# One encoder layer in split fp32r: the hi passes of a weight piece first, its lo passes last, and one score step moved up

## Chip, core and metric

The kernel runs on one core of one Trainium2 chip. The metric is device time in microseconds for one execution, the smaller the better. The inputs are drawn once, and the whole layer is computed in one launch.

## What is computed

One layer of a bidirectional encoder over 256 tokens of width 4096, all in float32:

```
h = layer_norm(x, emb_ln_g, emb_ln_b)
p = h @ w_in                      # 4096 x (4*2048 + 2048 + 512 + 512 + 2048)
y_conv = c_b * centred_short_conv(c_c * c_h, conv_w) * silu(c_z)
y_attn = banded_window_attention(a_q, a_k, a_v, sink) * silu(a_z)
y = concatenate([y_conv, y_attn]) @ w_out          # 4096 x 4096
out = layer_norm(2**0.25 * h + y, ln_g, ln_b)
```

The attention has 16 query heads and 4 key/value heads of size 128, a window of 128 tokens to both sides, a linear distance bias and a learned sink logit in each softmax. The convolution has three taps.

## The kernel before

**Split products.** TensorE multiplies fp32r operands. To keep float32 accuracy, each operand is split in two fp32r halves, hi and lo, and each product is three matmuls into the same PSUM accumulator: hi by hi, hi by lo, lo by hi. The stationary operand is a 128x128 block of the activations (`xT`, with the hi half in its first 256 columns and the lo half in the next 256). The moving operand is 128x256 out of a weight piece (`whi` and `wlo`).

**Pieces.** The weights come in pieces of 128x2048 from HBM into raw buffers (`w0` to `w2`, sometimes more). The work is a list of 376 steps, one for each piece: 302 for the input projection (26 chunks of 512 columns) and 74 for the output projection (7 chunks of 512 and 2 of 256). There are three kinds:

- a plain piece ("in", "out"): 4 blocks of 128 rows by 512 columns, 48 matmuls, written by `mm` (L251 to L253) and `mm_out` (L921 to L923);
- a half piece ("half"): 2 such blocks, 24 matmuls, also by `mm`;
- a pair ("pair", "opair"): one level of Winograd's form of Strassen's product over two blocks of rows, two column halves and two token halves. It has seven products instead of eight, 21 matmuls, written by `mm_pair` (L275 to L277), into the accumulators `acc` and `pacc`. VectorE first makes sums of the raw weights (`sums`, L183 to L185); sums of the activations lie in `SC`.

**Halves of a piece.** ScalarE copies the raw piece into `whi` (`split_hi`, L204), rounded to fp32r. VectorE subtracts this from the raw piece and gets `wlo` (`split_lo`, L208). There are three buffers each of `whi` and `wlo`. The raw buffer is free when `wlo` is made, and SyncE's queue then loads the next piece.

**Order.** It is written by hand: engines take their instructions in program order, and waits follow from the operands. At step j the matmuls of piece j are issued, then `split_hi(j + 3)`, then the other work that is due at step j (a table `later`, filled by `at`), then loads, `sums(j + 4)` and `split_lo(j + 3)`.

**Attention between the pieces.** Four heads at a time are worked off in the steps behind a chunk of queries. `SPREAD` names the step of each part: transposed queries (`q_tr`, `q_lo`) and for each head `scores` (L561 to L563), `s_add` (L568 and the two instructions behind it: bias, maximum, negation), `exps`, `recip`, `norms`, `p_tr` (L602: transposes of the probabilities, and L604, their hi half), `p_lo` (L609, their lo half), `pv` (L616 to L618, the product with v, six matmuls) and `out_z`. Scores, transposed probabilities and the output of `pv` share two PSUM buffers, `att`. Transposes of projections are on L491.

**End.** The output projection's last chunk is worked token half by token half, and the final normalisation is applied at once.

Of the kernel before, what the change touches and what calls it, by code (L numbers as in the profile page):

```python
# [8 lines left out]
F32 = mybir.dt.float32  # L9
# [5 lines left out]
P = 128  # L15
D = 4096
S = 256
KT = D // P
# [14 lines left out]
W = 512  # L33
PK = PIECE // W
# [6 lines left out]
HW = W // 2  # L41
# [46 lines left out]
def npairs(ci):  # L88
    return PAIRS[ci] if ci < OUT else OUT_ORDERS[ci - OUT].count("S")
# [11 lines left out]
def encoder_kernel(ctx: ExitStack, tc: tile.TileContext, x, emb_g, emb_b, wi, ws, conv_w, sink, wo, ln_g, ln_b, out):  # L101
    nc = tc.nc
# [5 lines left out]
    ps_acc = ctx.enter_context(tc.tile_pool(name="ps_acc", bufs=4, space=PSUM))  # L108
# [115 lines left out]
    xT = const.tile([P, KT, 2 * S], F32R, name="xT")  # L224
# [9 lines left out]
    acc = {}  # L234

    def mm(j):
        _, ci, q = steps[j]
        hi, lo = wh.pop(j), wl.pop(j)
        first = j == 0 or steps[j - 1][1] != ci
        last = j == N_IN - 1 or steps[j + 1][1] != ci  # L240
        pk, k0 = (2, 2 * q) if steps[j][0] == "half" else (PK, q * PK)
        for k in range(pk):
            kt = k0 + k
            for i in range(2):
                if first and k == 0:
                    acc[ci, i] = ps_acc.tile([P, W], F32, name="acc")
                a = acc[ci, i]
                xh, xl = xT[:, kt, i * P:(i + 1) * P], xT[:, kt, S + i * P:S + (i + 1) * P]
                for c in range(0, W, HW):
                    o, sl = a[:, c:c + HW], slice(k * W + c, k * W + c + HW)  # L250
                    nc.tensor.matmul(o, xh, hi[:, sl], start=(first and k == 0 and c == 0), stop=False)  # L251
                    nc.tensor.matmul(o, xh, lo[:, sl], start=False, stop=False)  # L252
                    nc.tensor.matmul(o, xl, hi[:, sl], start=False, stop=(last and k == PK - 1 and c > 0))  # L253

    pacc, SC = {}, None

    def mm_pair(j):


        _, ci, p = steps[j]  # L260
        hi, lo = (t.pop(j).rearrange("p (b w) -> p b w", w=HW) for t in (wh, wl))
        last = p == npairs(ci) - 1
        if p == 0:
            for k in range(2):
                pacc[ci, k] = ps_p.tile([P, 2, HW], F32, name="pacc")
        a, b = 2 * p, 2 * p + 1
        x = lambda kt, i: (xT[:, kt, i * HT:(i + 1) * HT], xT[:, kt, (2 + i) * HT:(3 + i) * HT])
        sc = lambda n: (SC[p][:, 0, n, :], SC[p][:, 1, n, :])
        p0, p1, c0, c1 = pacc[ci, 0], pacc[ci, 1], acc[ci, 0], acc[ci, 1]
        for (ah, al), w, o, opens, closes in (  # L270
                (x(a, 0), 2, p0[:, 0, :], True, False), (x(b, 0), 3, c0[:, 0:HW], False, False),
                (sc(2), 1, c0[:, HW:W], False, False), (x(b, 1), 7, c1[:, 0:HW], False, False),
                (sc(0), 5, p1[:, 1, :], True, False), (x(a, 1) if ci < OUT else sc(3), 6, p0[:, 1, :], False, True),
                (sc(1), 4, p1[:, 0, :], False, True)):
            nc.tensor.matmul(o, ah, hi[:, w, :], start=(opens and p == 0), stop=False)  # L275
            nc.tensor.matmul(o, ah, lo[:, w, :], start=False, stop=False)  # L276
            nc.tensor.matmul(o, al, hi[:, w, :], start=False, stop=(closes and last))  # L277


    def small_chain(i, dst):  # L280
# [10 lines left out]
    with tc.tile_pool(name="pro", bufs=1) as pro:  # L291
# [15 lines left out]
        first = [wpool.tile([P, PIECE + GAP], F32, name=f"first{j}", tag="whi")[:, OFF:OFF + PIECE] for j in range(2)]  # L307
# [117 lines left out]
        load(6)  # L425
        transp2(4)
        mm(2)
        turned2(4)
        x_split(4)
        split(4)  # L430
        load(7)
        transp2(5)
        mm(3)
        turned2(5)
        x_split(5)
        split(5)
        load(8)
        transp2(6)
        mm(4)
        turned2(6)  # L440
        x_split(6)
# [58 lines left out]
    v = pa.tile([P, 2, 2, 2, P], F32R, name="v")  # L500
# [110 lines left out]
    def pv(h):  # L611
        t, g = st_.pop(("pT", h))[0], h // GROUP % 2
        o_ps = st_["o", h] = ps_att.tile([P, S], F32, name="att")
        for kb in range(2):
            vh, vl = v[:, g, kb, 0, :], v[:, g, kb, 1, :]
            nc.tensor.matmul(o_ps, vh, t[:, 0, kb, :], start=(kb == 0), stop=False)  # L616
            nc.tensor.matmul(o_ps, vh, t[:, 1, kb, :], start=False, stop=False)
            nc.tensor.matmul(o_ps, vl, t[:, 0, kb, :], start=False, stop=(kb == 1))  # L618

    def out_z(h):  # L620
        y = st_["zT", h // GROUP][:, h % GROUP, :]
# [4 lines left out]
    def head(n, *steps):  # L626
        return [(t, f, n) for t, f in zip(steps, (scores, s_add, exps, recip, norms, p_tr, p_lo, pv, out_z))]

    SPREAD = [(6, q_tr, 0), (7, q_lo, 0), (10, q_tr, 1), (11, q_lo, 1)] + head(0, 8, 9, 9, 10, 10, 13, 15, 19, 20) + head(
        1, 9, 10, 10, 11, 12, 19, 21, 22, 23) + head(2, 13, 18, 18, 19, 20, 24, 27, 28, 29) + head(  # L630
        3, 21, 22, 22, 23, 23, 28, 30, 31, 32)

    def open_pc():
# [169 lines left out]
    for j in range(n_pro, N_IN):  # L803
        kind, ci, q = steps[j]
        if j == z0 + 4:
            extra.clear()
        if j == z0 + 12:
            extra.insert(0, (pw, "w6"))
        mm_pair(j) if kind == "pair" else mm(j)
        split_hi(j + 3)  # L810
        for fn, a in later.pop(j, []):
            fn(*a)
        if kind == "pair" and q == PAIRS[ci] - 1:
            pair_copy(ci)
            at(j + 1, pair_sums, ci)
        if j in X_SUMS:
            x_sums(X_SUMS.index(j), pa.tile([P, 4 * S], F32, name="xs", tag="zT", bufs=2))
        if steps[j + 1][1] != ci or j == N_IN - 1:
            if ci == c_ch0:
                at(j + 10, open_pc)  # L820
            if PAIRS[ci]:
                at(j + (4 if j < N_IN - 1 else 1), chunk_end, j + 1, ci)
            else:
                chunk_end(j, ci)
        loads(j)
        sums(j + 4)
        split_lo(j + 3)
# [79 lines left out]
    def mm_out(j, n, halves, k0=0, k1=None):  # L907
        c0, w, pk, j0 = chunks[n]
        ci, q = steps[j][1:]
        hi, lo = wh[j], wl[j]  # L910
        for k in range(k0, k1 or pk):
            s = q * pk + k
            first, last = j == j0 and k == 0, s == KT - 1
            for i in halves:
                if first:
                    acc[ci, i] = ps_acc.tile([P, 512], F32, name="acc")[:, 0:w]
                o = acc[ci, i]
                yh, yl = xT[:, s, i * P:(i + 1) * P], xT[:, s, S + i * P:S + (i + 1) * P]
                for c in range(0, w, HW):
                    oc, sl = o[:, c:c + HW], slice(k * w + c, k * w + c + HW)  # L920
                    nc.tensor.matmul(oc, yh, hi[:, sl], start=(first and c == 0), stop=False)  # L921
                    nc.tensor.matmul(oc, yh, lo[:, sl], start=False, stop=False)  # L922
                    nc.tensor.matmul(oc, yl, hi[:, sl], start=False, stop=(last and c + HW == w))  # L923

    def plus_res(n):

# [84 lines left out]
    for n, (c0, w, pk, j0) in enumerate(chunks):  # L1011
        us = out_units(n)
        np_ = sum(u[0] == "opair" for u in us)
        for t, (kind, _, q) in enumerate(us):
            j = j0 + t
            if kind == "opair":
                mm_pair(j)
            else:
                mm_out(j, n, (0,) if n == ncs - 1 else (0, 1))
# [35 lines left out]
    n = ncs - 1  # L1055
    r0 = finish_lhs(n, 0)
    mm_out(last_mm, n, (1,))
    mm_out(last_mm + 1, n, (1,))
    finish_tr(0)
    end_out2(n, 0, r0)  # L1060
# [73 lines left out]
```

## Time and profile before

| | |
|---|---|
| time, median of 3 runs | 1524.67 us (1524.48 to 1525.1) |
| profiled execution, its own time | 1524.95 us |
| its span, first to last instruction | 1523.2 us |
| granted TensorE clock, mean | 0.999 |
| ScalarE busy | 783.4 us (51%) |
| VectorE busy | 1329.8 us (87%) |
| HBM read over the span | 305.23 MB, 206 GB/s together with what is written |

In the profile, PE is TensorE's matmuls, PEld its weight loads, DVE VectorE, ACT ScalarE. Times are microseconds from the start of the span. A row of the timeline has the start, the length, the engine, the line of the kernel, the operation, its output and inputs, the shapes, how many were merged into the row, and in brackets the idle time ahead of it with what ended it. Matmuls are pipelined: the length of one reaches over the starts of the next two, so the step from start to start is what counts, not the length. The list of waits names who waited for whom, the total, how often, and the longest.

### The profile page before, as it was taken

Reading aid. Unit: us, or ns where it says so; the run is one execution under the profiler, and the core shown is the slowest. Engines: PE = TensorE matmul, PEld = TensorE weight load, DVE = VectorE, ACT = ScalarE, POOL = GpSimd, SP = SyncE. Lnnn points to the kernel's source line nnn. Section 1 sums busy time; section 2 is a strip of 40 time slices with the busy share of each in tenths; the row PEclk is TensorE's granted clock in tenths of the full one; section 3 lists DMA queues with packets and bytes.
Section 4 is the critical chain, followed back from the end, with each engine's and each line's share of the span. In section 5 each row is a group of like instructions: output and inputs, shape, how many; then the busy total and the mean of one; then the engine's idle time right before and its main releaser. Section 6 shows DMA issues by size and latency. Waiting matters only on the chain.

```text
span 1523.2 us, 29953 instructions
## 1 busy us (share of the span) xinstructions
PE 1501.5 (99%) x12947; PEld 1478.8 (97%) x12947; DVE 1329.8 (87%) x1555; ACT 783.4 (51%) x669; POOL 1.3 (0%) x7
## 2 busy tenths in 40 slices
PE   7999999999999999999999999999999999999998
PEld 4999999999999999999999999999999999999997
DVE  7769899899899899899898989999899688888876
ACT  4545546656566555545455455545456444443431
POOL 0000000000000000000000000000000000000000
PEclk9999999999999999999999999999999999999999
DMA  7555654656655555656556555556557756666563
GB/s 289 211 180 194 208 199 165 205 180 204 203 178 184 176 184 200 236 194 231 188 191 208 204 211 194 196 193 234 201 201 278 281 190 229 247 213 227 215 238 143
DMA packets 71748, 316.17 MB, mean 208 GB/s; under 512 B 8544, under 2 KB 12608, under 8 KB 50880
## 3 DMA queue, kind: packets, MB, share of 16 engines
q1 hardware_dynamic: 70608, 312.43, 58.7%
q8 instruction: 101, 1.65, 0.4%
q10 hardware_dynamic: 1008, 1.84, 0.3%
q14 instruction: 31, 0.25, 0.0%
HBM read 305.23 MB, written 8.91 MB: 206 GB/s over the span
## 4 chain that ended last, share of the span: by engine, by line
PE 79%; DVE 15%; ACT 3%; issue 2%; DMA 1%; SPq 0%; ACTq 0%; DVEq 0%
PE acc L252 13%; PE acc L253 12%; PE acc L251 12%; DVE wlo L208 9%; PE acc L922 6%; PE acc L923 6%; PE acc L921 6%; PE pacc L277 4%; PE pacc L276 4%; PE pacc L275 4%; PE acc L277 3%; PE acc L275 3%; PE acc L276 3%; ACT whi L204 3%; DVE w L183 2%
## 5 line engine op out<-in xcount | busy, mean ns | idle before, releaser
L204 ACT ACTIVATE whi<-w 128x2048 fp32r<-128x2048 f32 (+1 forms) x354 | 623.8, 1762 | 615.6 <-DVE w L185 220.0
L208 DVE TENSOR_TENSOR wlo<-w,whi 128x2048 fp32r<-128x2048 f32 (+1 forms) x354 | 736.7, 2083 | 121.9 <-ACT whi L204 121.3
L252 PE MATMUL acc<-wlo,xT 128*128 128x256 f32 x1976 | 547.7, 277 | 3.7 <-DVE wlo L208 3.2
L251 PE MATMUL acc<-whi,xT 128*128 128x256 f32 x1976 | 547.0, 277 | 0.0
L253 PE MATMUL acc<-whi,xT 128*128 128x256 f32 x1976 | 544.5, 276 | 0.0
L252 PEld LDWEIGHTS acc<-wlo,xT 128*128 128x128 f32 x1976 | 371.1, 188 | 8.7 <-DVE wlo L208 8.2
L251 PEld LDWEIGHTS acc<-whi,xT 128*128 128x128 f32 x1976 | 371.1, 188 | 0.0
L253 PEld LDWEIGHTS acc<-whi,xT 128*128 128x128 f32 x1976 | 371.0, 188 | 0.0
L922 PE MATMUL acc<-wlo,xT 128*128 128x256 f32 x848 | 233.5, 275 | 1.0 <-DVE wlo L208 1.0
L921 PE MATMUL acc<-whi,xT 128*128 128x256 f32 x848 | 233.6, 275 | 0.0
L923 PE MATMUL acc<-whi,xT 128*128 128x256 f32 x848 | 233.3, 275 | 0.0
L922 PEld LDWEIGHTS acc<-wlo,xT 128*128 128x128 f32 x848 | 159.2, 188 | 1.4 <-DVE wlo L208 1.4
L921 PEld LDWEIGHTS acc<-whi,xT 128*128 128x128 f32 x848 | 159.2, 188 | 0.4 <-issue 0.4
L923 PEld LDWEIGHTS acc<-whi,xT 128*128 128x128 f32 x848 | 159.2, 188 | 0.0
L183 DVE TENSOR_TENSOR w<-w 128x512 f32<-128x512 f32 x179 | 122.5, 684 | 8.0 <-DMA w<-in_ws 8.0
L275 PE MATMUL acc<-whi,xT 128*128 128x256 f32 x370 | 102.1, 276 | 0.0
L276 PE MATMUL acc<-wlo,xT 128*128 128x256 f32 x370 | 102.1, 276 | 0.0
L277 PE MATMUL acc<-whi,xT 128*128 128x256 f32 x370 | 102.0, 276 | 0.0
L275 PE MATMUL pacc<-whi,xT 128*128 128x256 f32 x350 | 98.1, 280 | 0.0
L276 PE MATMUL pacc<-wlo,xT 128*128 128x256 f32 x350 | 96.5, 276 | 0.0
L277 PE MATMUL pacc<-whi,xT 128*128 128x256 f32 x350 | 96.4, 276 | 0.0
L277 PE MATMUL pacc<-whi,SC 128*128 128x256 f32 x330 | 90.9, 275 | 0.0
(230 smaller groups left out, 2047.0 us busy)
## 6 DMA issues: line engine op xcount, KB each, us to landing
w<-in_wi SPq DMA_DIRECT2D x112, 1024.0 KB
w<-in_ws SPq DMA_DIRECT2D x202, 512.0 KB
w<-in_wo SPq DMA_DIRECT2D x41, 1024.0 KB
R<-in_wo SPq DMA_DIRECT2D x13, 1024.0 KB
x<-in_x SPq DMA_DIRECT2D x7, 512.0 KB
yl<-yd SPq DMA_DIRECT2D x7, 512.0 KB
xc<-in_x SPq DMA_DIRECT2D x14, 256.0 KB
R<-in_ws SPq DMA_DIRECT2D x6, 512.0 KB
```

Source lines behind the costliest of these rows:

```text
L183: nc.vector.tensor_tensor(s01, b22, b12.to_broadcast([P, 2, HW]), op=ALU.add)
L204: nc.scalar.activation(part(j, wh[j]), part(j, raw[j]), AF.Copy)
L208: nc.vector.tensor_tensor(part(j, wl[j]), part(j, raw[j]), part(j, wh[j]).bitcast(F32), op=ALU.subtract)
L251: nc.tensor.matmul(o, xh, hi[:, sl], start=(first and k == 0 and c == 0), stop=False)
L252: nc.tensor.matmul(o, xh, lo[:, sl], start=False, stop=False)
L253: nc.tensor.matmul(o, xl, hi[:, sl], start=False, stop=(last and k == PK - 1 and c > 0))
L275: nc.tensor.matmul(o, ah, hi[:, w, :], start=(opens and p == 0), stop=False)
L276: nc.tensor.matmul(o, ah, lo[:, w, :], start=False, stop=False)
L277: nc.tensor.matmul(o, al, hi[:, w, :], start=False, stop=(closes and last))
L921: nc.tensor.matmul(oc, yh, hi[:, sl], start=(first and c == 0), stop=False)
L922: nc.tensor.matmul(oc, yh, lo[:, sl], start=False, stop=False)
L923: nc.tensor.matmul(oc, yl, hi[:, sl], start=False, stop=(last and c + HW == w))
```

## The change

In `mm`, `mm_pair`, `mm_out` and `pv`, the loop over the halves of the moving operand becomes the outermost one. First come all matmuls of the step with the hi half as moving operand (with both the hi and the lo half of the stationary operand), then all with the lo half. Number and shapes stay. In `SPREAD`, `s_add` of head 2 goes from step 18 to step 17.

```diff
 def mm(j):                        # mm_out in the same way
-        for k in range(pk):
-            kt = k0 + k
...
-                for c in range(0, W, HW):
-                    o, sl = a[:, c:c + HW], slice(k * W + c, k * W + c + HW)
-                    nc.tensor.matmul(o, xh, hi[:, sl], start=(first and k == 0 and c == 0), stop=False)
-                    nc.tensor.matmul(o, xh, lo[:, sl], start=False, stop=False)
-                    nc.tensor.matmul(o, xl, hi[:, sl], start=False, stop=(last and k == PK - 1 and c > 0))
+        for w, offs in ((hi, (0, S)), (lo, (0,))):
+            for k in range(pk):
+                for i in range(2):
+                    for off in offs:
+                        x = xT[:, k0 + k, off + i * P:off + (i + 1) * P]
+                        for c in range(0, W, HW):
+                            nc.tensor.matmul(acc[ci, i][:, c:c + HW], x, w[:, k * W + c:k * W + c + HW],
+                                             start=(first and w is hi and k + off + c == 0),
+                                             stop=(last and w is lo and k == PK - 1 and c > 0))
 def mm_pair(j):
+        for (ah, al), w, o, opens, _ in products:
             nc.tensor.matmul(o, ah, hi[:, w, :], start=(opens and p == 0), stop=False)
-            nc.tensor.matmul(o, ah, lo[:, w, :], start=False, stop=False)
-            nc.tensor.matmul(o, al, hi[:, w, :], start=False, stop=(closes and last))
+            nc.tensor.matmul(o, al, hi[:, w, :], start=False, stop=False)
+        for (ah, _), w, o, _, closes in products:
+            nc.tensor.matmul(o, ah, lo[:, w, :], start=False, stop=(closes and last))
 def pv(h):
         for kb in range(2):
-            vh, vl = v[:, g, kb, 0, :], v[:, g, kb, 1, :]
-            nc.tensor.matmul(o_ps, vh, t[:, 0, kb, :], start=(kb == 0), stop=False)
-            nc.tensor.matmul(o_ps, vh, t[:, 1, kb, :], start=False, stop=False)
-            nc.tensor.matmul(o_ps, vl, t[:, 0, kb, :], start=False, stop=(kb == 1))
+            for part_ in range(2):
+                nc.tensor.matmul(o_ps, v[:, g, kb, part_, :], t[:, 0, kb, :], start=(kb + part_ == 0), stop=False)
+        for kb in range(2):
+            nc.tensor.matmul(o_ps, v[:, g, kb, 0, :], t[:, 1, kb, :], start=False, stop=(kb == 1))
 SPREAD
-        1, 9, 10, 10, 11, 12, 19, 21, 22, 23) + head(2, 13, 18, 18, 19, 20, 24, 27, 28, 29) + head(
+        1, 9, 10, 10, 11, 12, 19, 21, 22, 23) + head(2, 13, 17, 18, 19, 20, 24, 27, 28, 29) + head(
```

More of the change, by code (lines that the diff above doesn't have):

```diff
@@ L241, in mm @@
         pk, k0 = (2, 2 * q) if steps[j][0] == "half" else (PK, q * PK)
-        for k in range(pk):
-            kt = k0 + k
+        if first:
             for i in range(2):
[L245 to L248, printed above, removed]
-                for c in range(0, W, HW):
-                    o, sl = a[:, c:c + HW], slice(k * W + c, k * W + c + HW)
-                    nc.tensor.matmul(o, xh, hi[:, sl], start=(first and k == 0 and c == 0), stop=False)
-                    nc.tensor.matmul(o, xh, lo[:, sl], start=False, stop=False)
-                    nc.tensor.matmul(o, xl, hi[:, sl], start=False, stop=(last and k == PK - 1 and c > 0))
+                acc[ci, i] = ps_acc.tile([P, W], F32, name="acc")
+        for w, offs in ((hi, (0, S)), (lo, (0,))):
[7 more added lines that the diff above has]
+                                             stop=(last and w is lo and k == PK - 1 and c > 0))
     pacc, SC = {}, None
@@ L269, in mm_pair @@
         p0, p1, c0, c1 = pacc[ci, 0], pacc[ci, 1], acc[ci, 0], acc[ci, 1]
-        for (ah, al), w, o, opens, closes in (
+        products = (
                 (x(a, 0), 2, p0[:, 0, :], True, False), (x(b, 0), 3, c0[:, 0:HW], False, False),
@@ L273, in mm_pair @@
                 (sc(0), 5, p1[:, 1, :], True, False), (x(a, 1) if ci < OUT else sc(3), 6, p0[:, 1, :], False, True),
-                (sc(1), 4, p1[:, 0, :], False, True)):
+                (sc(1), 4, p1[:, 0, :], False, True))
+        for (ah, al), w, o, opens, _ in products:
             nc.tensor.matmul(o, ah, hi[:, w, :], start=(opens and p == 0), stop=False)
-            nc.tensor.matmul(o, ah, lo[:, w, :], start=False, stop=False)
-            nc.tensor.matmul(o, al, hi[:, w, :], start=False, stop=(closes and last))
+            nc.tensor.matmul(o, al, hi[:, w, :], start=False, stop=False)
+        for (ah, _), w, o, _, closes in products:
+            nc.tensor.matmul(o, ah, lo[:, w, :], start=False, stop=(closes and last))
     def small_chain(i, dst):
@@ L910, in mm_out @@
         hi, lo = wh[j], wl[j]
[L911 to L923, printed above, removed]
+        for m, offs in ((hi, (0, S)), (lo, (0,))):
+            for k in range(k0, k1 or pk):
+                s = q * pk + k
+                first, last = j == j0 and k == 0 and m is hi, s == KT - 1 and m is lo
+                for i in halves:
+                    if first:
+                        acc[ci, i] = ps_acc.tile([P, 512], F32, name="acc")[:, 0:w]
+                    for off in offs:
+                        y = xT[:, s, off + i * P:off + (i + 1) * P]
+                        for c in range(0, w, HW):
+                            nc.tensor.matmul(acc[ci, i][:, c:c + HW], y, m[:, k * w + c:k * w + c + HW],
+                                             start=(first and off + c == 0), stop=(last and c + HW == w))
     def plus_res(n):
```

## The prediction

> **What bounds the kernel now.** I read the page first, then stretches of the span, then the list of waits of the weight loads, then the order of time around single stalls. The page's first part says that TensorE is never free for long:
>
> ```profile
> PE 1501.5 (99%) x12947; PEld 1478.8 (97%) x12947; DVE 1329.8 (87%) x1555; ACT 783.4 (51%) x669; POOL 1.3 (0%) x7
> ```
>
> That share hides stalls, because each matmul is shown for about 0.28 us while the next starts 0.11 us later. So I count matmuls by stretch (columns: from:to, length, TensorE busy and its instructions, granted clock, DMA share, GB/s):
>
> ```profile
> 75.00:1175.00 1100.00, 1093.12 (x9519) 1.00 0.58 200
> ...
> 1190.00:1390.00 200.00, 200.00 (x1767) 1.00 0.63 226
> 1400.00:1500.00 100.00, 98.97 (x868) 1.00 0.59 210
> ```
>
> The second row is a stretch without idle time. A count takes in about two matmuls that only reach into the stretch, so its pace is 200 / 1765 = 0.1133 us. At this pace the 9517 matmuls of the first row need 1078.4 us, and 21.6 us are lost; the last row loses 100 - 866 x 0.1133 = 1.9 us. Together 23.5 us lie between this kernel and an uninterrupted stream, with the granted clock at 1.00 everywhere. Outside these stretches the change finds nothing to take (prologue, final normalisation).
>
> Where is it lost? The waits of the weight loads between 75 and 1503 us (total us, times, longest):
>
> ```profile
> PEld acc L252 <- DVE wlo L208: 8.2, 23, 0.9
> PEld att L602 <- PE att L618: 2.9, 4, 0.7
> PEld att L617 <- DVE pT L609: 2.0, 5, 0.8
> PEld acc L922 <- DVE wlo L208: 1.4, 2, 0.9
> ```
>
> The reader is to see that every entry but the second is a matmul with a lo half as its moving operand. L276, the lo pass of the pairs, is missing: pairs are never late. One stall in order of time:
>
> ```profile
> 670.19 0.28 PE L251 MATMUL acc<-whi,xT 128*128 128x256 f32 x1
> ...
> 671.13 0.39 PE L252 MATMUL acc<-wlo,xT 128*128 128x256 f32 x1 [0.67 <-DVE wlo L208]
> ...
> 671.35 0.28 PE L253 MATMUL acc<-whi,xT 128*128 128x256 f32 x1
> ```
>
> The piece begins with a hi matmul; the second is a lo matmul and stands 0.94 us behind it, and the third comes 0.22 us later. Two steps take 1.16 instead of 0.23 us: 0.93 lost, 0.07 more than the longest weight-load wait in the list. The other 46 matmuls of the piece, 31 of them hi, stand behind it.
>
> Two things look like stalls and stay. Behind a batch of transposes the record shows a step of 0.20:
>
> ```profile
> 235.34 0.60 PE L491 MATMUL att<-ident,q 128*128 128x128 f32 x4
> 235.70 0.36 PE L251 MATMUL acc<-whi,xT 128*128 128x256 f32 x1
> 235.90 0.28 PE L252 MATMUL acc<-wlo,xT 128*128 128x256 f32 x1
> ```
>
> From the first transpose to L252 are five steps in 0.56 us, 0.112 each, so nothing is lost: the L251 record only begins early. And the score products run at a slower pace without any wait:
>
> ```profile
> 229.03 0.28 PE L561 MATMUL att<-kT,qhl 128*128 128x256 f32 x1
> ...
> 230.93 0.28 PE L276 MATMUL acc<-wlo,xT 128*128 128x256 f32 x1
> ```
>
> That is 16 steps in 1.90 us, 0.1188 each. For 16 heads at 17 steps this is 16 x 17 x 0.0054 = 1.5 us. The same pace for some six matmuls behind each of about 50 transpose batches is an estimate of 1.6 us. So some 3 us of the 23.5 are not the change's.
>
> **The change part by part.**
>
> *Lo passes last in a piece.* Number and shape of the matmuls and weight loads stay. In a full piece (48 matmuls) the first lo matmul moves from place 2 to place 33, so lo may come 31 x 0.1133 = 3.5 us later; in a pair (21) from 2 to 15, 1.5 us; in a half piece (24) from 2 to 17, 1.7 us. The longest lateness is 0.94 us, so each listed wait falls inside. Price by the list: L252 and L922, 8.2 + 1.4 = 9.6 us, and 0.07 to 0.1 more for each of 25, 2.1 us: 11.7.
>
> What is late next? PE will reach the following lo sooner by what it no longer stalls, by estimate at most 1.3 us between two breathing spaces of VectorE (one stall of 0.93 and one of the list's mean length, 8.2 / 23 = 0.36). The tight places are pairs after a pair:
>
> ```profile
> 665.33 2.03 DVE L208 TENSOR_TENSOR wlo<-w,whi 128x1792 fp32r<-128x1792 f32 x1 [0.78 <-ACT whi L204]
> ```
>
> ```profile
> 667.81 0.28 PE L275 MATMUL pacc<-whi,xT 128*128 128x256 f32 x1
> 667.92 0.28 PE L276 MATMUL pacc<-wlo,xT 128*128 128x256 f32 x1
> ```
>
> Its lo half ends at 667.36, 0.56 before L276. Afterwards it has 0.56 + 1.5 = 2.0 us, more than 1.3. The cover holds.
>
> *Hi freed sooner.* The last reader of a hi half now stands at two thirds of the piece, so ScalarE's copy three pieces on, which needs that buffer, can begin up to 16 x 0.1133 = 1.8 us earlier (0.8 in a pair). VectorE gains from it where it waits for that copy:
>
> ```profile
> DVE wlo L208 <- ACT whi L204: 120.8, 91, 3.1
> ```
>
> The lo buffer is free only at the end of the piece, as before. I cost this at nothing by itself: it only makes VectorE earlier, which widens the cover.
>
> *Product with v.* The two matmuls with the lo half of the probabilities move from places 2 and 5 to 5 and 6 of six; lo may be 0.34 us later. The largest such stall:
>
> ```profile
> 583.21 0.28 PE L616 MATMUL att<-pT,v 128*128 128x256 f32 x1
> 584.07 0.39 PE L617 MATMUL att<-pT,v 128*128 128x256 f32 x1 [0.58 <-DVE pT L609]
> 584.29 0.28 PE L618 MATMUL att<-pT,v 128*128 128x256 f32 x1
> ```
>
> Here 1.08 - 0.23 = 0.85 us are lost. The 0.34 us alone leave half of it; VectorE, released sooner by the hi halves, should take most of the rest (up to 0.8 us behind a pair). Of 2.0 + 5 x 0.08 = 2.4 us in the list I take 2.2; at worst 1.4.
>
> *Score step sooner.* For the third head of each group, the addition (L568), maximum and negation move ahead of the sums and the lo half of the step before. It issues VectorE work only, no DMA, and is moved past no other queue.
>
> ```profile
> 264.85 0.68 DVE L183 TENSOR_TENSOR w<-w 128x512 f32<-128x512 f32 x1
> ...
> 266.37 2.29 DVE L208 TENSOR_TENSOR wlo<-w,whi 128x2048 fp32r<-128x2048 f32 x1
> 268.57 0.68 DVE L568 SCALAR_TENSOR_TENSOR s<-tab,att 128x512 f32<-128x512 f32 x1
> ```
>
> ```profile
> 268.58 0.28 PE L618 MATMUL att<-pT,v 128*128 128x256 f32 x1
> 269.39 0.63 PE L602 MATMUL att<-ident,p 128*128 128x128 f32 x4 [0.54 <-DVE s L568]
> ```
>
> The transposes of the second head need the PSUM buffer that L568 reads out; 0.81 - 0.12 = 0.7 us are lost, four times, 2.8 us. Moved, L568 starts at 264.85, 3.7 us sooner, and the stall goes. Behind it on VectorE now stand the sums and a lo half, later by about 1.5 us; that lo half belongs to the piece that starts about 269 and is first wanted 3.5 us after its start, so 270.2 is early enough.
>
> *Pace in the new order.* Hi next to hi with the other column half stands at every L253 to L251 border of today's stream; two lo matmuls side by side do not occur, so I bound them: 0.1188 from the score products, 0.112 from the transposes. For about 4100 lo matmuls that is between +22 and -5 us. I take 0.1133, the pace of the same shape from the same tiles, hence nothing.
>
> *Sum.* Lo 11.7, product 2.2, score step 2.8, and the slow pace for some six matmuls behind 30 stalls, 30 x 6 x 0.0054 = 1.0: 17.7 us. From the other side, 23.5 - 3.1 = 20.4 us are not accounted for by what stays; short waits missing from the list lie between. I take 19.5. The profiled execution took 1524.95 us (span 1523.2); 1505.4 remain, and as it lies 0.28 above the median of the runs, 1505.2.
>
> **Rivals.**
>
> *VectorE becomes the bound, half the gain.* Its load by stretch (TensorE, weight loads, VectorE follow the length):
>
> ```profile
> 232.00:325.00 93.00, 92.37 (x805) 92.00 (x804) 84.86 (x109) 58.97 (x66) 0.00 (x0) 1.00 0.56 186
> ...
> 1114.00:1175.00 61.00, 60.33 (x530) 60.07 (x529) 57.79 (x59) 33.63 (x23) 0.00 (x0) 1.00 0.68 250
> ```
>
> For it: 57.79 of 61 us at the end of the projection. Against: elsewhere 8 of 93 us are free and the stalls there cost 2 to 3. If half the stalls came back: 1524.7 - 9.8 = 1515.
>
> *Slower pace, slower kernel.* If lo beside lo ran at the 0.1188 us of the score products, the 4100 cost 22 us: 1505.2 + 22 = 1527. It decides from 19.5 / 4100 = 4.8 ns a matmul. Against it: matmuls with repeated and with changed weights, outputs and blocks all run at 0.1133 together.
>
> *Completion signals.* The earlier release of hi needs one more signal in each of 376 pieces. Today the last matmul of a piece carries one; behind it:
>
> ```profile
> 1259.81 0.28 PE L277 MATMUL pacc<-whi,SCy 128*128 128x256 f32 x1
> 1259.92 0.28 PE L921 MATMUL acc<-whi,xT 128*128 128x256 f32 x1
> ```
>
> No cost to the 0.01 us of the rows; at that bound 376 x 0.01 = 3.8 us, 1509. The Trainium skill, "TensorE: Matmul & The Clock Gate", section "The cost: per-tile semaphore tail", states that completion increments serialise at some 26 ns each. By that figure an estimate would be 376 x 0.0263 = 9.9 us, and 1515; the row does not bear it out for matmuls in a stream.
>
> *Nothing moves.* If the wait for lo were kept ahead of the whole piece, the time stays at 1524.7. Against: each matmul waits for its own operands today (L251 at 670.19 ran before lo was there).
>
> *All of the loss goes.* If the slow paces go too: 1524.7 - 23.5 = 1501, with a pace a little better 1500.
>
> **How the numbers follow.** Forecast 0.69 (its own range 1502 to 1510), half gain 0.10, slower pace 0.05, signals 0.04, nothing 0.04, all 0.08. A measurement here tells 0.2%, 3 us, from no change. Faster: 0.69 + 0.10 + 0.04 + 0.08 = 0.91; same 0.04; slower 0.05. The range from 1499.5 to 1512 holds forecast, signals, all, and a little of the half gain: over 8 in 10.
>
> **What would show it.** In the profile after, L252's and L922's successors for lo are not waited for on VectorE's account, L602 not on L568, and the product with v hardly; the stretch with all projection pieces counts 200 us per 1765 matmuls nearly throughout; VectorE waits less for ScalarE. A step above 0.114 us between lo matmuls, a new wait at the first hi matmul of a piece, or VectorE above 97% in a stretch would make me wrong.

## The result and the profile after

The changed kernel takes 1506.03 us (median of 4 runs, 1505.22 to 1506.11) against 1524.88 us before (4 runs, 1524.48 to 1525.23). The ratio is 0.9875, with a 95% interval from 0.9858 to 0.9892: faster by 1.25%, clear of the noise, and 0.8 us above the forecast of 1505.2. The profiled execution took 1505.99 us, its span is 1504.3 us, 18.9 us shorter than before.

The count of matmuls by stretch in the changed kernel (from:to, length, TensorE busy and its instructions, granted clock, DMA share, GB/s):

```profile
75.00:1160.00 1085.00, 1085.00 (x9539) 1.00 0.58 204
...
1175.00:1375.00 200.00, 200.00 (x1767) 1.00 0.64 226
1385.00:1485.00 100.00, 100.00 (x883) 1.00 0.58 203
```

The second row has the same 1767 as its counterpart before, so the pace of 0.1133 us did not change. At this pace the first row loses 1085 - 9537 x 0.1133 = 4.5 us and the last 0.2. Before, 23.5 us were lost. The difference, 18.8, is the gain in the span to 0.1 us: the change took idle time from TensorE and nothing else.

In the list of waits of the changed kernel between 75 and 1480 us, neither matmuls nor weight loads wait for anyone. The first row of its list of VectorE's waits stands beside the 120.8 us of before:

```profile
DVE wlo L208 <- ACT whi L204: 82.0, 61, 3.1
```

VectorE waits less for ScalarE's copies, because these begin sooner. The piece that lost 0.93 us before starts at 662.77 in the changed kernel. VectorE's row for its lo half, and TensorE's rows around its start:

```profile
660.49 2.28 DVE L208 TENSOR_TENSOR wlo<-w,whi 128x2048 fp32r<-128x2048 f32 x1
```

```profile
662.66 0.28 PE L279 MATMUL pacc<-wlo,SC 128*128 128x256 f32 x1
662.77 0.50 PE L251 MATMUL acc<-whi,xT 128*128 128x256 f32 x3
```

The lo half is ready at 662.77, when its piece starts. In the kernel before it was ready at 671.07, 0.88 us after the start of the piece at 670.19:

```profile
668.79 2.28 DVE L208 TENSOR_TENSOR wlo<-w,whi 128x2048 fp32r<-128x2048 f32 x1
```

So two things happened at this place. The lo half is now wanted 3.6 us after the start instead of 0.1, and it also comes 0.88 us sooner relative to it. Which of the two made the gain is what the experiments ask. Below, cover is the time by which a lo half may come behind the start of its piece before TensorE waits for it.

### The profile page after: what moved, and what is told of

The parts are those of the page before. It is cut to its first block, busy times and chain, and to the rows that moved or that the text cites. A ratio compares the mean times of both kernels' runs of the same rounds, so it can differ in the third digit from the quotient of the medians.

```text
span 1504.3 us, 30113 instructions
## 1 busy us (share of the span) xinstructions
PE 1490.8 (99%) x12947; PEld 1475.4 (98%) x12947; DVE 1329.7 (88%) x1555; ACT 781.7 (52%) x669; POOL 1.3 (0%) x7
## 4 chain that ended last, share of the span: by engine, by line
PE 98%; DVE 1%; DMA 0%; ACT 0%; SPq 0%; issue 0%; ACTq 0%
PE acc L251 45%; PE acc L923 20%; PE pacc L276 6%; PE pacc L277 6%; PE pacc L279 6%; PE acc L277 4%; PE acc L276 4%; PE acc L279 4%; PE att L493 1%; PE att L618 1%; DVE st L330 0%; PE att L604 0%; PE acc L380 0%; DMA x<-in_x 0%; PE att L363 0%; DVE x L338 0%
## 5 line engine op out<-in xcount | busy, mean ns | idle before, releaser
L251 PE MATMUL acc<-whi,xT 128*128 128x256 f32 x3952 | 474.0, 276 | 0.0
L251 PEld LDWEIGHTS acc<-whi,xT 128*128 128x128 f32 x3952 | 459.9, 188 | 0.0
L251 PE MATMUL acc<-wlo,xT 128*128 128x256 f32 x1976 | 245.8, 275 | 0.0
L251 PEld LDWEIGHTS acc<-wlo,xT 128*128 128x128 f32 x1976 | 234.0, 188 | 0.0
L923 PE MATMUL acc<-whi,xT 128*128 128x256 f32 x1696 | 201.8, 275 | 0.0
L923 PEld LDWEIGHTS acc<-whi,xT 128*128 128x128 f32 x1696 | 196.6, 188 | 0.4 <-issue 0.4
L923 PE MATMUL acc<-wlo,xT 128*128 128x256 f32 x848 | 105.3, 275 | 0.0
L276 PE MATMUL acc<-whi,xT 128*128 128x256 f32 x370 | 102.1, 276 | 0.0
L277 PE MATMUL acc<-whi,xT 128*128 128x256 f32 x370 | 102.1, 276 | 0.0
L923 PEld LDWEIGHTS acc<-wlo,xT 128*128 128x128 f32 x848 | 100.4, 188 | 0.0
L279 PE MATMUL acc<-wlo,xT 128*128 128x256 f32 x370 | 92.8, 275 | 0.0
L277 PE MATMUL pacc<-whi,SC 128*128 128x256 f32 x330 | 91.0, 276 | 0.0
L276 PE MATMUL pacc<-whi,SC 128*128 128x256 f32 x330 | 91.0, 276 | 0.0
L279 PE MATMUL pacc<-wlo,SC 128*128 128x256 f32 x330 | 82.9, 275 | 0.0
L184 DVE TENSOR_TENSOR w<-w 128x256 f32<-128x256 f32 x179 | 76.1, 425 | 6.2
L185 DVE TENSOR_TENSOR w<-w 128x256 f32<-128x256 f32 x179 | 76.1, 425 | 6.2
```

What stands on the lines that cost most here:

```text
L184: nc.vector.tensor_tensor(r(6), r(5), r(1), op=ALU.add)
L185: nc.vector.tensor_tensor(r(7), r(6), r(3), op=ALU.add)
L251: nc.tensor.matmul(acc[ci, i][:, c:c + HW], x, w[:, k * W + c:k * W + c + HW], start=(first and w is hi and k + off + c == 0), stop=(last ...
L277: nc.tensor.matmul(o, al, hi[:, w, :], start=False, stop=False)
L279: nc.tensor.matmul(o, ah, lo[:, w, :], start=False, stop=(closes and last))
L923: nc.tensor.matmul(acc[ci, i][:, c:c + HW], y, m[:, k * w + c:k * w + c + HW], start=(first and off + c == 0), stop=(last and c + HW == w))
```

## Experiments

All times are medians beside runs of the kernel before on the same chip. The kernel before had a median of 1524.24 us beside `step18`, `only17`, `pairs_old` and `pv_old`, 1524.05 beside `hi_held`, `held_old`, `lo_second` and `per_block`, 1524.54 beside the others, and 1524.88 beside the changed kernel. It moves by 0.8 us itself, so differences of that size from the changed kernel's 1506.0 are read from the lists of waits and the rows, not from the times; under half a microsecond they are taken as none.

**The score step taken back (`step18`).**

```diff
-head(2, 13, 17, 18, 19, 20, 24, 27, 28, 29)
+head(2, 13, 18, 18, 19, 20, 24, 27, 28, 29)
```

> The changed kernel with the third head's score step back at step 18. My theory (VectorE works in order, the score addition holds the PSUM buffer for the transposes of the second head, 0.7 us in each of four groups): 2.8 us slower than the changed kernel, about 1508.8, and the wait of the transposes on the addition is back four times. Rival (the earlier release of hi alone had made VectorE early enough): no difference, 1506.0.

Measured: 1505.84 us, ratio 0.9877 (0.9864 to 0.9891). The rival holds: no difference. The rows of this kernel, VectorE first, then TensorE, for the same place as in the prediction:

```profile
265.53 0.68 DVE L570 SCALAR_TENSOR_TENSOR s<-tab,att 128x512 f32<-128x512 f32 x1
```

```profile
266.23 0.64 PE L618 MATMUL att<-pT,v 128*128 128x256 f32 x4
266.70 0.41 PE L620 MATMUL att<-pT,v 128*128 128x256 f32 x2
266.94 0.60 PE L604 MATMUL att<-ident,p 128*128 128x128 f32 x4
```

With the addition still behind the lo half, it begins 1.41 us ahead of the transposes. Before, it began only 0.12 us ahead of the place where they could have started (268.57, against 268.58 plus a step of 0.11). VectorE had come nearer without this edit.

**The score step alone (`only17`).** The kernel before, with the same line changed from 18 to 17.

> The kernel before with the score step alone moved to 17. My theory: 2.8 us faster than before, about 1522.1, the wait of the transposes on the addition gone. Rival (the lo half pushed back behind the addition now comes late instead, since it is still wanted at the second matmul of its piece): a new stall of up to 1 us in each of four groups at the piece behind the transposes, so between 1522 and 1526.

Measured: 1526.21 us, ratio 1.0012 (1.0003 to 1.0021): about 2 us slower. My theory falls, and the rival was too mild. The list of weight-load waits of this kernel from 75 to 1503 us:

```profile
PEld acc L252 <- DVE wlo L208: 12.4, 27, 1.1
PEld att L617 <- DVE pT L609: 2.0, 5, 0.8
PEld acc L922 <- DVE wlo L208: 1.3, 2, 0.8
```

The wait of the transposes (2.9 us in the list before) is gone, but the waits for lo went from 8.2 to 12.4. One place, TensorE:

```profile
268.53 0.60 PE L602 MATMUL att<-ident,p 128*128 128x128 f32 x4
268.88 0.36 PE L251 MATMUL acc<-whi,xT 128*128 128x256 f32 x1
270.11 0.39 PE L252 MATMUL acc<-wlo,xT 128*128 128x256 f32 x1 [0.86 <-DVE wlo L208]
```

The transposes follow at once, and the piece behind them waits about 1.0 us for its lo half, which now stands behind the addition, where it had lost 0.7 us before the transposes. The step pays only where lo has cover, and where hi is freed sooner as well (`step18`) it isn't needed.

**The pairs in the old order (`pairs_old`).** `mm_pair` as before, the rest as changed.

> The changed kernel with the pairs alone in the old order, lo second in each product. My theory (pairs are never late: the lo half lay 0.36 us or more ahead of its first reader before): no loss from pairs themselves, 1506 to 1506.5. Rival (it was the earlier release of hi in the pairs that let VectorE catch up, or with no stalls elsewhere the pairs become the late ones): waits on the lo half at the second matmul of pairs, up to 1 us in each of some 30 places of the projection, 1510 or more.

Measured: 1507.19 us, ratio 0.9887 (0.9874 to 0.9901), 1.2 us slower than the changed kernel, between the two theories and near mine. Its list of weight-load waits from 75 to 1480 us has two rows on VectorE:

```profile
PEld att L618 <- DVE pT L609: 0.4, 1, 0.4
PEld pacc L276 <- DVE wlo L208: 0.2, 1, 0.2
```

The list explains about half of the 1.2 us. The steps from start to start show the rest. The product with v loses 0.5 us once. Pairs are late at five places, by 0.1 to 0.3 us each and 0.8 us together (worked out from TensorE's rows; the list has only the longest). This is the longest:

```profile
637.23 0.28 PE L275 MATMUL pacc<-whi,xT 128*128 128x256 f32 x1
637.55 0.38 PE L276 MATMUL pacc<-wlo,xT 128*128 128x256 f32 x1
637.78 0.28 PE L277 MATMUL pacc<-whi,xT 128*128 128x256 f32 x1
```

Two steps take 0.55 instead of 0.23 us. So pairs, which were never late before, are now a little late at some places: this is the mechanism of the rival, at a small part of its size. That VectorE lost the sooner release of hi in the pairs would explain why the product with v waits again; this is argued, not shown.

**The product with v in the old order (`pv_old`).** `pv` as before, the rest as changed.

> The changed kernel with the product with v alone in the old order. My theory: the lo half of the probabilities is wanted 0.34 us sooner, and of the 2.4 us that were lost there before most come back: 1507.5 to 1508.4. Rival (VectorE is so much earlier through the hi halves that the lo half of the probabilities is in time in either order): 1506.0 to 1506.4.

Measured: 1506.04 us, ratio 0.9879 (0.9866 to 0.9893). No difference, and no wait in its lists from 75 to 1480 us. The rival holds: the lo half of the probabilities is in time in either order.

**Late lo passes with hi held (`hi_held`).** In the list of a piece's or pair's matmuls, in the changed order, with n of them on hi:

```diff
-return mms
+return mms[:n - 1] + mms[n:] + [mms[n - 1]]
```

> The changed kernel, but of the hi matmuls of each piece and pair the last one stands behind the lo passes: lo is wanted as late as in the changed kernel (one matmul sooner), while the hi buffer is freed at the end of the piece as before. My theory (the waits for lo go because lo is wanted later; VectorE then runs at the distance to TensorE that it had before): waits for lo gone, about 0.5 to 0.9 us left at the product with v, 1506.5 to 1507. Rival (the sooner release of hi is what does it): waits for lo and others come back, 1512 or more.

Measured: 1506.18 us, ratio 0.9881 (0.9867 to 0.9896), no difference from the changed kernel and a little better than I expected. The place of the long stall in this kernel, VectorE and then TensorE:

```profile
661.57 2.29 DVE L213 TENSOR_TENSOR wlo<-w,whi 128x2048 fp32r<-128x2048 f32 x1
```

```profile
662.98 3.67 PE L254 MATMUL acc<-whi,xT 128*128 128x256 f32 x31
666.49 0.73 PE L254 MATMUL acc<-wlo,xT 128*128 128x256 f32 x5
```

The lo half ends at 663.86, 0.88 us behind the start of its piece, exactly the lateness of before, and TensorE wants it at 666.49. Late lo passes alone hide it. The one wait on VectorE in its lists from 75 to 1480 us is at the product with v, where my theory had put what is left:

```profile
PEld att L626 <- DVE pT L617: 0.4, 1, 0.4
```

**The same, with score step and product with v as before (`held_old`).** The kernel before with the order of `hi_held` in pieces and pairs.

> As the kernel that holds hi, and besides with the score step at 18 and the old order in the product with v, so that only the late lo passes are left of the change. My theory, formed after these two were found to cost nothing in the changed kernel (the sooner release of hi let VectorE reach the score addition and the lo half of the probabilities earlier): with hi held, both waits are back, 2.8 + 2.4 us, so 1510.5 to 1511.5. Rival (it was enough that TensorE no longer stalls for lo, or their waits were only a consequence of those): 1506 to 1507.

Measured: 1511.13 us, ratio 0.9914 (0.9899 to 0.9929). My theory holds in number and place; the list of its weight-load waits:

```profile
PEld att L610 <- PE att L626: 2.8, 4, 0.7
PEld att L625 <- DVE pT L617: 2.0, 5, 0.8
```

These are the two rows of before, hardly changed, and no row for lo is left. So the late lo passes by themselves take 13 us (1511.1 instead of 1524.05), all of the waits for lo and nothing else. The two small edits then take 5 us more.

**Hi freed sooner, lo wanted as soon as before (`lo_second`).**

```diff
-return mms
+return mms[:1] + [mms[n]] + mms[1:n] + mms[n + 1:]
```

> The changed kernel, but one lo matmul of each piece and pair stands at the second place, the other lo matmuls last: lo is wanted as soon as before, hi is freed at two thirds. My theory: of the 13 to 14 us of waits for lo that stood in the kernel before, VectorE's earlier start takes 0.5 to 1 us off each late place, so some 4 to 7 us stay, at four or five long places above all: 1510 to 1513. Rival one (the release of hi does everything): 1506. Rival two (it does nothing for lo, VectorE is full in the stretches ahead of the late places): 1518 to 1520.

Measured: 1507.88 us, ratio 0.9892 (0.9875 to 0.9908). Only 1.9 us of the gain are missing, less than my theory and far less than the second rival expected. The place of the long stall:

```profile
662.98 0.28 PE L254 MATMUL acc<-whi,xT 128*128 128x256 f32 x1
663.15 0.38 PE L254 MATMUL acc<-wlo,xT 128*128 128x256 f32 x1
663.37 0.40 PE L254 MATMUL acc<-whi,xT 128*128 128x256 f32 x2
```

Two steps take 0.39 us: 0.16 lost, where 0.93 were lost before. Eight places in the projection still lose 0.1 to 0.2 us each in this way, 1.2 us together (worked out from TensorE's rows); the other 0.7 us are not traced. The lo half of this piece is ready at 663.10, 0.12 us behind the start instead of 0.88:

```profile
660.82 2.28 DVE L213 TENSOR_TENSOR wlo<-w,whi 128x2048 fp32r<-128x2048 f32 x1
```

VectorE's chain ahead of this place begins at a copy that waited for a hi buffer, in the kernel before as

```profile
644.93 1.93 ACT L204 ACTIVATE whi<-w 128x2048 fp32r<-128x2048 f32 x1 [0.55 <-PE acc L253]
```

so the sooner release moves the whole chain, 26 us long up to the end of the lo half at 671.07. Behind the wait for this copy VectorE is idle only once in it, for 0.78 us at 665.33 (the row is in the prediction), and that wait is for a copy (at 663.58) that had to follow VectorE's own sums (up to 663.41).

**Only the release of hi (`hi_only`).** As the last one, with score step and product with v as before.

> Only the sooner release of hi is left of the change: one lo matmul of each piece and pair stands second, the other lo matmuls last, and the score step (18) and the product with v are as before. My theory, formed after the second-place kernel took 1507.9: VectorE, released 0.8 us sooner at each place, reaches the score addition and the lo half of the probabilities in time, so 1507.8 to 1508.5. Rival (those two waits need the late lo passes as well, since lo at the second place lets TensorE wait and shifts both engines together): 1510 to 1513.

Measured: 1508.0 us, ratio 0.9891 (0.9878 to 0.9905). The one wait of its weight loads on VectorE from 75 to 1490 us:

```profile
PEld acc L254 <- DVE wlo L213: 0.2, 1, 0.2
```

My theory holds. The sooner release of hi takes 16.5 us alone (1508.0 instead of 1524.54), the waits at the score addition and the product with v among them.

**Hi and lo passes for each block (`per_block`).** In `mm` and `mm_out`, the loops over k and over the halves change places.

```diff
-for w, offs in ((hi, (0, S)), (lo, (0,))):
-    for k in range(pk):
+for k in range(pk):
+    for w, offs in ((hi, (0, S)), (lo, (0,))):
```

> The changed kernel, but in plain and half pieces the order is hi passes, then lo passes, for each block of 128 rows: lo is first wanted at the ninth matmul instead of the 33rd (0.8 us later than before instead of 3.5), hi is freed four matmuls before the end instead of 16. Pairs, product with v and score step as changed. My theory (the longest lateness was 0.94 us, so 0.8 us of cover is nearly enough): four or five stalls of 0.15 to 0.25 us, 1506.5 to 1507.5. Rival (without the stalls VectorE falls further behind than the old lateness, so that the long cover is needed): 1509 or more.

Measured: 1505.89 us, ratio 0.9879 (0.9866 to 0.9894). Not even the 0.5 us of my theory: no wait is left in its lists from 75 to 1480 us. 0.8 us of cover and a hi buffer freed 0.45 us sooner in plain pieces are enough, but only just: at one piece the lo half came 0.23 us ahead of its first reader (worked out from the rows of VectorE and TensorE).

**More work for VectorE (`after_load`, `per_block_load`).**

```diff
+    idle = small.tile([P, 1], F32, name="idle", bufs=1)
+
+    def extra_work(j):
+        if j % 2 == 0:
+            nc.vector.tensor_reduce(idle, ident, axis=AX.X, op=ALU.max)
...
         sums(j + 4)
+        extra_work(j)
         split_lo(j + 3)
```

> The changed kernel with one more VectorE instruction, a maximum over 128x128 that nobody reads (about 0.2 us), ahead of the lo half in every second step of the input projection: 148 of them, some 30 us of VectorE's time, whose load in the projection goes from 92% to about 94%. My theory (a cover of 3.5 us in plain pieces and 1.5 in pairs absorbs it): 1506.0 to 1506.5. Rival (VectorE is near enough to its limit that it becomes the bound in some stretches): 1508 or more.

> The same additional VectorE work in the kernel with hi and lo passes for each block, whose cover in plain pieces is 0.8 us and whose lo halves came up to 0.75 us behind the start of their pieces. My theory (the short cover is used up nearly everywhere): stalls of 0.1 to 0.5 us at the late places, 1507.5 to 1510. Rival (VectorE catches up between the late places, the cover lasts): 1506 to 1506.5, as without the work.

Measured: 1525.01 us (ratio 1.0003, 0.9994 to 1.0012) and 1524.93 us (1.0002, 0.9993 to 1.0011), some 19 us slower than without. Three of the four expectations fall by their numbers. The fourth, the rival of `after_load` (1508 or more), is met in number but not in cause: VectorE is not the bound and the cover has nothing to do with it, for neither list has a wait of TensorE from 75 to 1490 us. In `after_load` TensorE ran at a slower pace, in the output projection too, where no instruction was added:

```profile
L215 DVE TENSOR_REDUCE idle<-ident 128x1 f32<-128x128 f32 x147 | 40.9, 278 | 0.0
```

```profile
75.00:1160.00 1085.00, 1085.00 (x9397) 1.00 0.58 198
1175.00:1375.00 200.00, 200.00 (x1755) 1.00 0.64 233
```

In the second stretch 1755 matmuls stand where 1767 stood. The time lies in the pairs: against the changed kernel, the steps of the pairs take 15.8 us more, those of the plain and half pieces of the projection 2.3, and all others together hardly anything (worked out from the starts of the matmuls from 75 to 1480 us). The additional tile of four bytes a partition moves what the program places behind it. In the built program the sums of the activations that only pairs read (`SC`, and `SCy` in the output projection) lie 32 bytes further on in each partition, while `xT`, `whi` and `wlo` keep their places. Here are the first and the last of seven lo matmuls of a pair in this kernel, and below them in the changed kernel:

```profile
647.96 0.28 PE L285 MATMUL pacc<-wlo,xT 128*128 128x256 f32 x1
...
648.66 0.28 PE L285 MATMUL pacc<-wlo,SC 128*128 128x256 f32 x1
```

```profile
641.24 0.28 PE L279 MATMUL pacc<-wlo,xT 128*128 128x256 f32 x1
...
641.92 0.28 PE L279 MATMUL pacc<-wlo,SC 128*128 128x256 f32 x1
```

Six steps take 0.70 us here and 0.68 there, 0.117 against 0.113. No added instruction runs in the output projection, so that the place of the tiles makes the difference is the reading that is left there. No run has the tile without the instructions, so this is not shown, and what the cover can bear was not measured.

**Other operands for the scores (`scores_x`).** Queries and keys are left out of the scores; both operands come from `xT`.

```diff
-qh, ql = q[:, 0, a, b * P:(b + 1) * P], q[:, 1, a, b * P:(b + 1) * P]
+qh, ql = xT[:, 30, b * P:(b + 1) * P], xT[:, 30, S + b * P:S + (b + 1) * P]
```

> The changed kernel with other operands in the score products: both come from the activations' tile, which the weight pieces use too, so that queries and keys are left out of the scores; number, shape and place of the matmuls stay. It asks why score products and the matmuls behind them run at 0.119 instead of 0.1133 us. If the place or the content of the query and key tiles makes it: 0.1133 at the scores, about 1.5 us less, 1504.5. If it comes from the change to another output bank or from standing between two pieces: no difference, 1506.0, and the pace of 0.119 stays.

Measured: 1505.95 us, ratio 0.9878 (0.9865 to 0.9892). The slower pace at the scores stays, 16 steps in 1.90 us as before:

```profile
227.35 0.28 PE L563 MATMUL att<-xT 128*128 128x256 f32 x1
...
229.25 0.28 PE L276 MATMUL pacc<-whi,xT 128*128 128x256 f32 x1
```

So it comes neither from the place nor from the content of query and key tiles. Its cause is open.

## Why the prediction was right, and where it was not

| kernel | lo wanted late | hi freed sooner | score step, product with v | us |
|---|---|---|---|---|
| before | no | no | old | 1524.1 to 1524.9 |
| `only17` | no | no | score step new | 1526.2 |
| `held_old` | yes | no | old | 1511.1 |
| `hi_held` | yes | no | new | 1506.2 |
| `hi_only` | no | yes | old | 1508.0 |
| `lo_second` | no | yes | new | 1507.9 |
| `step18`, `pv_old` | yes | yes | one old | 1505.8, 1506.0 |
| changed | yes | yes | new | 1506.0 |

- **What bounds the kernel, and the loss of 23.5 us:** right. The gain is the fall of this loss to 4.7 us.
- **Lo passes last, 11.7 us and 1.0 for the slow pace behind stalls:** right by itself. `held_old` took 13 us and every wait for lo. With the other two terms, and hi held, `hi_held` comes to 1506.2: the three terms of the sum are enough by themselves.
- **Hi freed sooner, costed at nothing:** this step failed, although the total didn't show it. By itself it is worth 16.5 us (`hi_only`), more than the late lo passes. I saw that VectorE gains 0.8 to 1.8 us in each place from it, but took it as cover only, and did not set it against latenesses of up to 0.94 us, which it nearly removes.
- **Product with v, 2.2 us, and score step, 2.8 us:** the waits went and were as large as said (`held_old`: 4.9 us between 1511.1 and 1506.2), but in the changed kernel these edits do nothing (`pv_old`, `step18`). The changed kernel has two causes for the same gain, and either nearly suffices: the three terms of the sum without the release of hi (1506.2), or the release of hi without them (1508.0). The total came out right because each wait was counted once, under an edit that would have removed it, while the release of hi removed nearly all of them anyway.
- **The lo half pushed behind the score addition:** right that it needs cover. Without it the push costs more than the step brings (`only17`).
- **What is late next, at most 1.3 us:** in `hi_held`, the latest lo half of the projection came 1.28 us behind the start of its piece, and one of the output projection 1.45 us, behind sums that had waited for their weights (worked out from the ends of VectorE's instructions and the starts of the pieces). The cover of 3.5 us held. In the changed kernel itself, no lo half was later than 0.4 us.
- **Pace in the new order, 0.1133:** right, 1767 in 200 us in both kernels. The rival of a slower pace falls, and so does that of completion signals: in the trace 798 matmuls of this shape carry a signal instead of 418, and in the stretch of 200 us 91 instead of 48, with the same count of matmuls. The Trainium skill ("TensorE: Matmul & The Clock Gate", section "The cost: per-tile semaphore tail") states some 26 ns for each increment in the tail behind tiled matmuls. In this stream no such cost appears: by that figure, an estimate, the additional 43 would take 1.1 us of the stretch, ten matmuls.
- **VectorE as the bound:** not here. Its share in the projection rose from 992.85 of 1100 us to 994.01 of 1085, 91.6%, and TensorE waits for nothing. How much more it could bear stays open.
- **What stays, 3.1 us:** undersized; 4.7 us stay. The product with v runs at the slow pace too, which I left out: in the rows of `step18`, six matmuls from 266.23 reach to 266.94, 0.118 each. By the starts of the changed kernel's matmuls, the scores and the eleven matmuls behind them lose 1.8 us (I had 1.5), the transposes and those behind them 1.1 (I had 1.6), the product with v and those behind it 1.0 and all others 0.5 (I had neither): 4.4 us of the 4.7.
- **All of the loss goes, nothing moves:** both rivals fall. The slow pace stayed, and the hi matmuls of a piece ran ahead of its lo half (31 of them in `hi_held`, from 662.98 on, with lo ready at 663.86).

## What to carry to other kernels

When a matmul engine waits briefly for an operand that another engine makes from one of two halves, order the passes so that the half which comes first is used first: it wants the late half later, and it also frees the early half's buffer sooner, which here pulled the whole chain behind it forward. Several edits that each remove the same short waits don't add up: price each against the lead that the others already give, and test each alone and left out. A move that gains at one place may push something else behind it, so a step that is harmless with cover can cost time without it.

## What the runs showed of the hardware

Two things were new to me. A maximum over 128x128 every second step and its result tile of four bytes a partition came with 19 us more and not a single wait of TensorE: the pairs of matmuls, which read the sums of the activations, ran slower throughout (9397 matmuls in 1085 us instead of 9539), in the stretch without additional instructions too (1755 in 200 us instead of 1767). That the moved tiles did it is likely from this stretch, but not shown. And the matmuls at the score products and the product with v, and some ten behind the scores, take 0.119 us instead of 0.1133, with no wait, with either of the two sets of operands that were tried at the scores.
